# A two-layer hybrid encoder in fp32: first gate/up tile in step with the input, last down tile and final norm in two halves of the tokens

## The chip, the cores and the metric

The kernel runs on one core of one Trainium2 chip. The metric is the device time of one execution in microseconds (us), the median of several runs. Engines are named by the profile's letters: PE is TensorE (matmuls; PEld its weight loads), ACT is ScalarE, DVE is VectorE, POOL is GpSimd, SP is SyncE, which issues the DMAs.

## The reference

One sequence of 512 tokens of 1024 features goes through two layers and a final norm. Four mixers run side by side in a layer: a short convolution, an RWKV-7 scan in both directions, retention, and latent attention (MLA).

```python
for l in range(DEPTH):
    x = x + 0.5 * swiglu(rmsnorm(x, ffn1_norm[l]), ffn1_w_gate[l], ffn1_w_up[l], ffn1_w_down[l])
    u = rmsnorm(x, mix_norm[l]) @ w_in[l]
    ...
    x = x + jnp.concatenate([y_conv, y_rwkv, y_ret, y_mla], axis=-1) @ w_out[l]
    x = x + 0.5 * swiglu(rmsnorm(x, ffn2_norm[l]), ffn2_w_gate[l], ffn2_w_up[l], ffn2_w_down[l])
return rmsnorm(x, final_norm)
```

`swiglu` is `(silu(x @ w_gate) * (x @ w_up)) @ w_down` with 2816 hidden features; `rmsnorm` divides by the root of the mean square over the features and multiplies with a gain.

## The kernel before, in words

x is kept transposed in SBUF as eight tiles x[0] to x[7], each 128 features by 512 tokens. To keep fp32 accuracy every matrix product is made of three matmuls (`mm3`, L336 to L340): high part of the weights times high part of x, high times low, low times high. Weights come from memory in raw fp32 tiles (`load`, a ring of two); `split` (L320) casts a tile to its high part on ACT (L327) and subtracts to get the low part on DVE (L328), each into a ring of two. `norm_part` (L258 on) makes the high part of a scaled x tile, xg, on ACT (L273) and its low part on DVE (L274); `norm_square` squares x on ACT and adds up on POOL; `norm_sum` sums over features on PE (tile st) and takes the inverse root in small DVE steps (`rsqrt`); `norm_spread` broadcasts that row on PE (tile pb) and copies it (rb).

`ffn` (L343) runs, for each half of the hidden features, eleven gate/up tiles (PSUM tiles pg and pu, 24 matmuls each) and eight down tiles (pd, 33 matmuls each). Ahead of it, `setup` issues the first transfers on SP in the order x[0], first 512 columns of the first gate/up tile, x[1] to x[3], the next 512, x[4] to x[7], the other 1024 columns. After the last down tile the final norm squares the last x tile, sums, spreads, and multiplies eight tiles, six on DVE and two on POOL, each followed by its output transfer (main program, L1192 to L1199).

`Mixers.run` makes the projections (`proj`, PSUM tile pj, 24 matmuls of 128x512 each), and for retention's and RWKV's natural layout `proj_nat` (L490 on): pn, 128 tokens by 288 columns, whose weights come as raw pieces of 2 x 576 columns, two such pairs, k tiles 0 to 3 and 4 to 7. `rwkv_inverse` solves small triangular systems: its input NR goes through memory (DMAs s<-NR, L957), comes back as Lb (L959) and Nb (L962); ACT copies Lb reversed into one half of Nb (L960); then DVE runs 31 steps of a product tmpR (L972) and a subtraction from Rb (L974); the result returns through memory, and two sets of small matmuls (psY, psR) use it.

The order of instructions on each engine is not the order of the source: the Tile scheduler sets it (L1271), from its own simulated timeline and priorities (`high_priority` in `split`, `issue_after` where the source wants an order). Each engine then runs its own list in that order.

Of the kernel before, what the change touches and what calls it, by code (L numbers as in the profile page):

```python
# [134 lines left out]
class K:  # L135
# [17 lines left out]
    def setup(self):  # L153
# [15 lines left out]
        first = self.ring.tile([P, 2048], F32, name="w_raw", tag="w_raw", bufs=2)  # L169
        self.first = first  # L170
        for d in range(KD):
            nc.sync.dma_start(self.x[d], I["xT"][:, d, :])
            if d in (0, 3):
                q = 512 * (d // 3)
                nc.sync.dma_start(first[:, q:q + 512], I["gu1"][0, 0][:, q:q + 512])
        nc.sync.dma_start(first[:, 1024:2048], I["gu1"][0, 0][:, 1024:2048])
        self.con_t = per.tile([P, I["con"].shape[1]], F32, name="con_t")
# [80 lines left out]
    def norm_part(self, d, gain, l, square=True):  # L258

        nc, V, A = self.nc, self.nc.vector, self.nc.scalar  # L260
        x = self.x[d]
        if d == 0:
            self.acc = self.ft("acc")
            self.xh, self.xl, self.xo = [], [], []
        if gain == "final_norm":
            self.norm_square(d, True)
            o = self.ft("o")
            A.activation(o, x, AF.Copy, scale=self.v(gain, 0, d))
            self.xo.append(o)
            return  # L270
        hl = self.ht(f"xg{d}", dt=F32R)
        g = self.v(gain, l, d)
        A.activation(hl[:, 0], x, AF.Copy, scale=g)  # L273
        V.scalar_tensor_tensor(hl[:, 1], x, g, hl[:, 0].bitcast(F32), ALU.mult, ALU.subtract)  # L274
        self.xh.append(hl[:, 0])
        self.xl.append(hl[:, 1])
        if square:
            self.norm_square(d)

    def norm_square(self, d, last=False):  # L280
        nc, A, x = self.nc, self.nc.scalar, self.x[d]
        if d == 0:
            A.activation(self.acc, x, AF.Square)
        else:
            self.sq = self.ft("sq")
            A.activation(self.sq, x, AF.Square)
            if d < KD - 1 or not last:
                nc.gpsimd.tensor_tensor(self.acc, self.acc, self.sq, ALU.add)

    def norm_sum(self, last=False):  # L290

        nc = self.nc
        acc = self.acc
        ps = self.ps("st", "a")
        for i, a in enumerate((acc, self.sq)[:1 + last]):
            for tt in range(NT):
                c = NT * i + tt
                m = nc.tensor.matmul(ps[:, c:c + 1], a[:, P * tt:P * tt + P], self.con("ones"), start=True, stop=True)
        rn = self.tmp.tile([P, NT], F32, name="rn", tag="rn")
        ss = ps[:, 0:NT]  # L300
        if last:
            ss = self.tmp.tile([P, NT], F32, name="ss", tag="m_s2", bufs=1)
            nc.vector.tensor_copy(ss, ps[:, 0:NT])
            nc.vector.tensor_tensor(ss, ps[:, NT:2 * NT], ss, ALU.add)
        self.rsqrt(rn, ss, NT, 1.0 / D, EPS)
# [12 lines left out]


# [21 lines left out]


    def ffn(self, l, which, then, between=None):  # L343
        nc, V, A = self.nc, self.nc.vector, self.nc.scalar
        wgu, wdn = self.I[f"gu{which}"], self.I[f"dn{which}"]
        for half in range(2):
            gh, gl = [], []
            for f in range(HALF):
# [5 lines left out]
                pu = self.ps("pu", "b")  # L354
                for o, ps in ((0, pg), (1, pu)):
                    hi, lo = self.split(raw[:, 1024 * o:1024 * o + 1024], 1024, 512 if begin else 1024)
                    if begin and o == 1:
                        with self.tc.issue_after(self.split_hi.ins):
                            for d in range(KD):
                                self.norm_square(d)  # L360
                    for k in range(KD):
# [820 lines left out]
def body(tc, I, out, dbg=None, layers=L):  # L1182
    with ExitStack() as ctx:
        k = K(ctx, tc, I, out, dbg)
        k.setup()
        for d in range(KD):
            k.norm_part(d, "ffn1_norm", 0, square=False)
        for l in range(layers):
            k.ffn(l, 1, ("mix_norm", l), between=k.rope_tables if l == 0 else None)
            Mixers(k, l).run()  # L1190
            k.ffn(l, 2, ("ffn1_norm", l + 1) if l < layers - 1 else ("final_norm", 0))
        k.norm_sum(last=True)  # L1192
        k.norm_spread(last=True)
        for d in range(KD):
            if d in (2, 5):
                k.nc.gpsimd.tensor_tensor(k.x[d], k.xo[d], k.rb, ALU.mult)
            else:
                k.nc.vector.tensor_tensor(k.x[d], k.xo[d], k.pb, ALU.mult)
            k.nc.sync.dma_start(out[:, d, :], k.x[d])  # L1199

# [75 lines left out]
```

## Time and profile before

| what | value |
|---|---|
| median of 3 runs | 2170.99 us (2170.92 to 2171.12) |
| profiled execution | 2169.86 us; its span 2168.1 us |
| PE busy | 2131.3 us, 98% of the span |
| DVE, ACT, POOL busy | 51%, 33%, 6% |
| mean granted PE clock | 0.995 |
| DMA | 204.68 MB, mean 94 GB/s |

The page was taken from one execution. Its busy time of PE is a model (matmuls overlap; one of 512 columns lasts 0.39 us and the next starts 0.23 us later). Times in the timelines are us from the start of the span.

### The profile page before, as it was taken

The page shows a single profiled execution, that of the slowest core. Times are in us where ns is not written, and L with a number is a line of the kernel's source. Part 1 is how long each engine was busy: PE and PEld are TensorE (multiplying, and loading weights), DVE is VectorE, ACT ScalarE, POOL GpSimd, SP SyncE. Part 2 cuts the span into 40 slices and gives each one's busy share as a digit, 9 for nine tenths or more (in the row PEclk, how much of TensorE's full clock was granted, in tenths as well). Part 3 has the DMA queues.
Part 4 walks back from the last instruction along what each step waited for, and adds up shares of the span by engine and source line. Part 5 has one row for each costly group of instructions (what it writes and reads, how often), then busy time and mean ns, then how long its engine had stood idle before and what let it go on. Part 6 is the DMA issues. An engine that isn't in the chain of part 4 may idle for free.

```text
span 2168.1 us, 27576 instructions
## 1 busy us (share of the span) xinstructions
PE 2131.3 (98%) x11316; PEld 1714.9 (79%) x11316; DVE 1113.3 (51%) x1917; ACT 711.6 (33%) x1061; POOL 122.4 (6%) x146
## 2 busy tenths in 40 slices
PE   8999999999999999999999999999999999999997
PEld 7888888788666888888888888887886578888886
DVE  4454445676577543443544444457756865434433
ACT  4222223443233422222322222335323243222232
POOL 2000001000020100000100000010001210000001
PEclk9999999999999999999999999999999999999998
DMA  4223224144002322322322232242330122223222
GB/s 170 97 85 106 98 95 151 61 118 129 20 21 86 116 98 85 117 97 79 106 97 91 94 109 95 92 147 72 116 101 21 64 90 105 91 80 111 97 87 79
DMA packets 65294, 204.68 MB, mean 94 GB/s; under 512 B 26512, under 2 KB 26768, under 8 KB 50960
## 3 DMA queue, kind: packets, MB, share of 16 engines
q1 hardware_dynamic: 65168, 202.93, 28.5%
q8 instruction: 88, 1.44, 0.3%
q14 instruction: 38, 0.31, 0.0%
HBM read 191.37 MB, written 9.44 MB: 93 GB/s over the span
## 4 chain that ended last, share of the span: by engine, by line
PE 93%; DVE 4%; ACT 1%; DMA 1%; issue 1%; SPq 0%; DVEq 0%; ACTq 0%
PE pg L338 7%; PE pg L340 7%; PE pg L339 7%; PE pu L338 7%; PE pd L340 7%; PE pu L339 7%; PE pd L339 7%; PE pd L338 7%; PE pu L340 7%; PE pj L338 4%; PE pj L339 4%; PE pj L340 4%; PE po L338 1%; PE po L339 1%; PE po L340 1%; PE m_pq L758 1%
## 5 line engine op out<-in xcount | busy, mean ns | idle before, releaser
L327 ACT CAST w_hi<-w_raw 128x1024 fp32r<-128x1024 f32 (+4 forms) x446 | 367.4, 836 | 1132.1 <-PE pg L339 308.9
L328 DVE TENSOR_TENSOR w_lo<-w_raw,w_hi 128x1024 fp32r<-128x1024 f32 (+4 forms) x446 | 425.7, 962 | 229.4 <-ACT w_hi L327 220.1
L338 PE MATMUL pg<-xg,w_hi 128*128 128x512 f32 x704 | 275.5, 391 | 6.2 <-ACT w_hi L327 6.2
L340 PE MATMUL pg<-xg,w_lo 128*128 128x512 f32 x704 | 275.0, 391 | 0.0
L339 PE MATMUL pg<-xg,w_hi 128*128 128x512 f32 x704 | 274.9, 390 | 0.0
L338 PE MATMUL pu<-xg,w_hi 128*128 128x512 f32 x704 | 274.1, 389 | 0.4 <-ACT w_hi L327 0.4
L339 PE MATMUL pu<-xg,w_hi 128*128 128x512 f32 x704 | 274.2, 389 | 0.0
L340 PE MATMUL pu<-xg,w_lo 128*128 128x512 f32 x704 | 273.9, 389 | 0.0
L340 PE MATMUL pd<-g,w_lo 128*128 128x512 f32 x704 | 273.9, 389 | 0.0
L338 PE MATMUL pd<-g,w_hi 128*128 128x512 f32 x704 | 273.9, 389 | 0.0
L339 PE MATMUL pd<-g,w_hi 128*128 128x512 f32 x704 | 273.9, 389 | 0.0
L372 DVE TENSOR_TENSOR g<-pu,s 128x512 f32<-128x512 f32 x88 | 60.9, 692 | 274.0 <-PE pu L340 271.2
L369 DVE TENSOR_TENSOR s<-pg,rb 128x512 f32<-128x512 f32 x88 | 60.8, 691 | 206.5 <-PE pg L340 206.4
L338 PEld LDWEIGHTS pg<-xg,w_hi 128*128 128x128 f32 x704 | 132.7, 188 | 33.7 <-ACT w_hi L327 6.2
L340 PEld LDWEIGHTS pg<-xg,w_lo 128*128 128x128 f32 x704 | 132.7, 188 | 28.5 <-DVE w_lo L328 1.0
L339 PEld LDWEIGHTS pg<-xg,w_hi 128*128 128x128 f32 x704 | 132.7, 188 | 28.0 <-DVE xg L274 0.5
L338 PEld LDWEIGHTS pu<-xg,w_hi 128*128 128x128 f32 x704 | 132.2, 188 | 28.1 <-ACT w_hi L327 0.9
L340 PEld LDWEIGHTS pu<-xg,w_lo 128*128 128x128 f32 x704 | 132.2, 188 | 27.5 <-DVE w_lo L328 0.2
L339 PEld LDWEIGHTS pd<-g,w_hi 128*128 128x128 f32 x704 | 132.2, 188 | 27.5
L338 PEld LDWEIGHTS pd<-g,w_hi 128*128 128x128 f32 x704 | 132.2, 188 | 27.4
L340 PEld LDWEIGHTS pd<-g,w_lo 128*128 128x128 f32 x704 | 132.2, 188 | 27.4
L339 PEld LDWEIGHTS pu<-xg,w_hi 128*128 128x128 f32 x704 | 132.2, 188 | 27.3
(294 smaller groups left out, 2706.5 us busy)
## 6 DMA issues: line engine op xcount, KB each, us to landing
w_raw<-gu SPq DMA_DIRECT2D x87, 1024.0 KB, 4.8
w_raw<-dn SPq DMA_DIRECT2D x64, 704.0 KB, 4.2
w_raw<-win SPq DMA_DIRECT2D x22, 1024.0 KB, 5.1
w_raw<-wo SPq DMA_DIRECT2D x32, 256.0 KB, 2.8
xs<-x SPq DMA_DIRECT2D x16, 256.0 KB, 4.7
x<-xs SPq DMA_DIRECT2D x16, 256.0 KB, 5.7
w_raw<-wtv SPq DMA_DIRECT2D x4, 576.0 KB, 4.2
x<-xT SPq DMA_DIRECT2D x8, 256.0 KB, 5.9
```

Source lines behind the costliest of these rows:

```text
L327: self.split_hi = self.nc.scalar.copy(hi[:, s], raw[:, s])
L328: self.nc.vector.tensor_tensor(lo[:, s], raw[:, s], hi[:, s].bitcast(F32), ALU.subtract)
L338: T_.matmul(ps, hi, xh, start=start, stop=False)
L339: T_.matmul(ps, hi, xl, start=False, stop=False)
L340: T_.matmul(ps, lo, xh, start=False, stop=stop)
L369: V.tensor_tensor(s, pg, rb, ALU.mult)
L372: V.tensor_tensor(g, pu, s, ALU.mult)
L758: mm(pq, wq[i][:, P * h:P * h + P], qa[i], start=i == 0, stop=i == 2)
```

## The change

Front: the first tile's gate and up weights come in three pieces each (columns 0 to 256, 256 to 512, 512 to 1024) between the x tiles, and a new function `ffn_begin` runs gate and up in step over k, with `norm_part(k)` just ahead of each use and the squares after the last cast. End: the last down tile of the last layer is computed for tokens 0 to 255 and then 256 to 511, each followed by a new function `end` with that half's sum, norm, products and output transfers (128 KB each). The special cases for the last norm disappear.

```diff
+        pieces = {0: (0, 256), 2: (256, 512), 4: (512, 1024)}
         for d in range(KD):
             nc.sync.dma_start(self.x[d], I["xT"][:, d, :])
-            if d in (0, 3):
-                q = 512 * (d // 3)
-                nc.sync.dma_start(first[:, q:q + 512], I["gu1"][0, 0][:, q:q + 512])
-        nc.sync.dma_start(first[:, 1024:2048], I["gu1"][0, 0][:, 1024:2048])
+            if d in pieces:
+                a, b = pieces[d]
+                for o in (0, 1024):
+                    nc.sync.dma_start(first[:, o + a:o + b], I["gu1"][0, 0][:, o + a:o + b])
...
+    def end(self, c, pd):
...
+        V.scalar_tensor_tensor(t, pd, 0.5, self.rb[:, s], ALU.mult, ALU.mult)
+        V.tensor_tensor(x, x, t, ALU.add)
+        A.activation(sq, x, AF.Square)
+        A.activation(o, x, AF.Copy, scale=self.v("final_norm", 0, d))
+        ps = self.ps("st", "mm")
+        for a in (self.acc, self.sqe):
+            for i in range(2):
+                q = 256 * c + P * i
+                nc.tensor.matmul(ps[:, i:i + 1], a[:, q:q + P], self.con("ones"), start=a is self.acc and i == 0,
+                                 stop=True, skip_group_check=True)
+        rn = self.tmp.tile([P, NT], F32, name="rn", tag="rn")
+        self.rsqrt(rn[:, 0:2], ps[:, 0:2], 2, 1.0 / D, EPS)
+        pb = self.ps("pb", "mm")
+        for i in range(2):
+            nc.tensor.matmul(pb[:, P * i:P * i + P], rn[:, i:i + 1].to_broadcast([P, P]), self.con("ident"),
+                             start=True, stop=True)
+        fb = self.last_t[:, s]
+        A.copy(fb, pb[:, 0:256])
+        for d in range(KD):
+            if d in (1, 4):
+                G.tensor_tensor(self.x[d][:, s], self.xo[d][:, s], fb, ALU.mult)
+            else:
+                V.tensor_tensor(self.x[d][:, s], self.xo[d][:, s], pb[:, 0:256], ALU.mult)
+            nc.sync.dma_start(self.out[:, d, s], self.x[d][:, s])
...
+    def ffn_begin(self, raw, banks):
...
+        for a, b in ((0, 256), (256, 512), (512, 1024)):
+            for o, (hi, lo) in enumerate(w):
+                r = raw[:, 1024 * o + a:1024 * o + b]
+                last = nc.scalar.copy(hi[:, a:b], r)
+                nc.vector.tensor_tensor(lo[:, a:b], r, hi[:, a:b].bitcast(F32), ALU.subtract)
+            for k in range(a // P, b // P):
+                if k:
+                    self.norm_part(k, "ffn1_norm", 0, square=False)
+                for (hi, lo), ps in zip(w, banks):
+                    self.mm3(ps, hi[:, P * k:P * k + P], lo[:, P * k:P * k + P], self.xh[k], self.xl[k],
+                             k == 0, k == KD - 1)
+        with self.tc.issue_after(last.ins):
+            for d in range(KD):
+                self.norm_square(d)
...
+                if half == 1 and d == KD - 1 and then[0] == "final_norm":
+                    w = [self.split(raw[:, P * a:P * b], P * (b - a)) for a, b in ((0, 6), (6, HALF))]
+                    for c in range(2):
+                        pd = self.ps("pd", "a")[:, 0:256]
+                        s = slice(256 * c, 256 * c + 256)
+                        for k in range(HALF):
+                            hi, lo = w[k // 6]
+                            q = P * (k % 6)
+                            self.mm3(pd, hi[:, q:q + P], lo[:, q:q + P], gh[k][:, s], gl[k][:, s], k == 0, k == HALF - 1)
+                        self.end(c, pd)
+                    return
```

The scheduler's order of the instructions changes in places that the diff does not name. Three of them follow. Line numbers of the changed kernel are 25 higher in `split` (L352, L353) and 57 higher in the mixers.

First, the mixers of layer 0 (layer 1 alike): ACT's list around the copy Nb<-Lb of `rwkv_inverse`; the casts of 128x576 are the two pairs of pn's weights. Before:

```order
L327 CAST w_hi<-w_raw 128x576 [waits DMAHW4_49,DVE_49,PE_49]
L327 CAST w_hi<-w_raw 128x576
L684 ACTIVATE m_lat<-pj,vec 128x512 [waits PE_49]
L686 ACTIVATE m_sq<-pj 128x512
L327 CAST w_hi<-w_raw 128x576 [waits DMAHW5_49,DVE_49,PE_49]
L327 CAST w_hi<-w_raw 128x576
L684 ACTIVATE m_lat<-pj,vec 128x512 [waits PE_49]
L686 ACTIVATE m_sq<-pj 128x512
L960 COPY Nb<-Lb 64x1024 [waits DMAHW6_49]
```

With the change:

```order
L352 CAST w_hi<-w_raw 128x576 [waits DMAHW7_49,DVE_49,PE_49]
L352 CAST w_hi<-w_raw 128x576
L741 ACTIVATE m_lat<-pj,vec 128x512 [waits PE_49]
L743 ACTIVATE m_sq<-pj 128x512
L1017 COPY Nb<-Lb 64x1024 [waits DMAHW1_49,DVE_49]
L352 CAST w_hi<-w_raw 128x576 [waits DMAHW0_49,DVE_49,PE_49]
L352 CAST w_hi<-w_raw 128x576
L741 ACTIVATE m_lat<-pj,vec 128x512 [waits PE_49]
L743 ACTIVATE m_sq<-pj 128x512
```

The copy, which waits for a DMA, has moved ahead of the second pair of casts and of the second m_lat and m_sq. On DVE at the same place the list has, with the change:

```order
L353 TENSOR_TENSOR w_lo<-w_raw,w_hi 128x576 [waits DMAHW7_49,PE_49,Activation_49]
L353 TENSOR_TENSOR w_lo<-w_raw,w_hi 128x576 [waits Activation_49]
L1002 TENSOR_TENSOR NR_3056<-psN,con_t 128x8x64 [waits PE_49] x2
L1002 TENSOR_TENSOR NR_3057<-psN,con_t 128x8x64 [waits PE_49] x2
L1029 TENSOR_TENSOR tmpR<-Nb,Rb 128x31 [waits DMAHW2_49,Activation_49,Pool_49]
L1031 TENSOR_TENSOR Rb<-Rb,tmpR 128x31 [waits DVE_49]
L353 TENSOR_TENSOR w_lo<-w_raw,w_hi 128x576 [waits DMAHW0_49,PE_49,Activation_49]
L1029 TENSOR_TENSOR tmpR<-Nb,Rb 128x60 [waits DVE_49]
L353 TENSOR_TENSOR w_lo<-w_raw,w_hi 128x576 [waits Activation_49]
```

Before, the second pair of w_lo stood ahead of the first tmpR, directly behind NR; now each of the two stands behind a product of the inverse.

Second, the start: ACT's list behind the last casts of the first tile's weights (xg_166, xg_175 and xg_184 are made from x[5] to x[7]). Before:

```order
L273 ACTIVATE xg_121<-x_81,vec 128x512 [waits DMAHW2_49]
L327 CAST w_hi<-w_raw 128x512 [waits DMAHW3_49]
L327 CAST w_hi<-w_raw 128x512
L283 ACTIVATE acc<-x_74 128x512
L286 ACTIVATE sq<-x_75 128x512
```

With the change:

```order
L379 CAST w_hi<-w_raw 128x512 [waits DMAHW3_49]
L284 ACTIVATE acc<-x_74 128x512
L287 ACTIVATE sq<-x_75 128x512
L287 ACTIVATE sq<-x_76 128x512
L287 ACTIVATE sq<-x_77 128x512
L287 ACTIVATE sq<-x_78 128x512
L274 ACTIVATE xg_166<-x_79,vec 128x512 [waits DMAHW4_49]
L287 ACTIVATE sq<-x_79 128x512
L274 ACTIVATE xg_175<-x_80,vec 128x512 [waits DMAHW5_49]
L287 ACTIVATE sq<-x_80 128x512
L274 ACTIVATE xg_184<-x_81,vec 128x512 [waits DMAHW6_49]
L287 ACTIVATE sq<-x_81 128x512
```

The squares, which all stood behind the last xg and the last cast, now stand partly between the last three xg.

Third, the end: PE's list, with the change (st is the sum over features, sqe the last tile's square, pb the broadcast):

```order
L365 MATMUL pd<-g_15481,w_lo 128x256
L327 MATMUL st<-con_t,sqe 128x1 [waits Activation_49]
L327 MATMUL st<-con_t,sqe 128x1
L333 MATMUL pb<-con_t,rn 128x128 [waits DVE_49]
L333 MATMUL pb<-con_t,rn 128x128
L327 MATMUL st<-con_t,acc 128x1 x2
L327 MATMUL st<-con_t,sqe 128x1 [waits Activation_49]
L327 MATMUL st<-con_t,sqe 128x1
L333 MATMUL pb<-con_t,rn 128x128 [waits DVE_49,PE_49]
L333 MATMUL pb<-con_t,rn 128x128
```

The first row is the last matmul of the second half; the two st and two pb behind it belong to the first half, and the rest to the second. Before, the list ended with pd, eight st and four pb of all tokens.

## Rows read from the trace of the kernel before

**Rows 1.** The page, part 4: chain that ended last, by engine

```profile
PE 93%; DVE 4%; ACT 1%; DMA 1%; issue 1%; SPq 0%; DVEq 0%; ACTq 0%
```

**Rows 2.** Timelines of ACT and PE at the start (start us, us, engine, line, operation)

```profile
10.15 2.73 ACT L273 ACTIVATE xg<-x,vec 128x512 fp32r<-128x512 f32 x4
13.43 1.14 ACT L327 CAST w_hi<-w_raw 128x512 fp32r<-128x512 f32 x2 [0.55 <-DMA w_raw<-gu]
...
15.01 3.74 ACT L286 ACTIVATE sq<-x 128x512 f32<-128x512 f32 x7
18.66 1.03 ACT L327 CAST w_hi<-w_raw 128x1024 fp32r<-128x1024 f32 x1
...
21.02 0.50 PE L338 MATMUL pu<-xg,w_hi 128*128 128x512 f32 x1 [0.44 <-ACT w_hi L327]
```

**Rows 3.** Windows: stretch, its us, busy PE PEld DVE ACT POOL, PEclk, DMA share, GB/s

```profile
8.00:12.00 4.00, 4.00 (x11) 2.91 (x11) 3.46 (x6) 3.37 (x6) 0.00 (x0) 1.00 1.04 379
```

**Rows 4.** Timelines of ACT, DVE and PE in layer 0's mixers

```profile
460.37 1.25 ACT L327 CAST w_hi<-w_raw 128x576 fp32r<-128x576 f32 x2 [5.42 <-PE pj L339]
...
467.02 1.05 ACT L960 COPY Nb<-Lb 64x1024 f32<-64x1024 f32 x1 [4.33 <-DMA Lb<-s]
...
461.07 1.43 DVE L328 TENSOR_TENSOR w_lo<-w_raw,w_hi 128x576 fp32r<-128x576 f32 x2 [3.92 <-ACT w_hi L327]
468.31 0.21 DVE L972 TENSOR_TENSOR tmpR<-Nb,Rb 128x31 f32<-128x31 f32 x1 [5.81 <-DMA Nb<-s]
...
463.59 0.43 PE L502 MATMUL pn<-w_hi,xg 128*128 128x288 f32 x2
...
475.90 0.50 PE L340 MATMUL pj<-xg,w_lo 128*128 128x512 f32 x1 [1.72 <-DVE w_lo L328]
```

**Rows 5.** The same in layer 1's mixers

```profile
1537.56 1.04 ACT L960 COPY Nb<-Lb 64x1024 f32<-64x1024 f32 x1 [3.19 <-DMA Lb<-s]
...
1535.27 0.43 PE L502 MATMUL pn<-w_hi,xg 128*128 128x288 f32 x2
...
1546.50 0.50 PE L340 MATMUL pj<-xg,w_lo 128*128 128x512 f32 x1 [1.01 <-DVE w_lo L328]
```

**Rows 6.** The page, part 6: DMA issues, count, KB each, us to landing

```profile
w_raw<-win SPq DMA_DIRECT2D x22, 1024.0 KB, 5.1
```

**Rows 7.** Windows around idle PE and at a low clock

```profile
474.00:476.00 2.00, 0.28 (x2) 0.10 (x1) 2.00 (x5) 0.88 (x2) 0.00 (x0) 1.00 0.00 0
...
537.00:543.50 6.50, 6.50 (x20) 5.11 (x19) 0.27 (x1) 0.81 (x3) 2.76 (x5) 0.50 0.18 68
...
1608.50:1612.00 3.50, 3.50 (x11) 2.70 (x10) 0.00 (x0) 0.60 (x1) 1.18 (x1) 0.55 0.07 23
...
2151.00:2155.00 4.00, 1.61 (x14) 1.44 (x13) 2.02 (x7) 1.24 (x2) 0.00 (x0) 0.99 0.00 0
2155.00:2160.00 5.00, 2.07 (x8) 1.78 (x8) 1.91 (x11) 0.58 (x1) 0.39 (x1) 0.50 0.00 0
```

**Rows 8.** Timelines of PE, DVE and SP at the end

```profile
2150.38 0.40 PE L340 MATMUL pd<-g,w_lo 128*128 128x512 f32 x1
2150.61 0.95 PE L298 MATMUL st<-con_t,acc 128*128 128x1 f32 x8
...
2156.84 2.07 PE L246 MATMUL pb<-con_t,rn 128*128 128x128 f32 x8 [2.84 <-DVE rn L241]
...
2154.04 0.16 DVE L303 COPY ss<-st 128x4 f32<-128x4 f32 x1 [1.81 <-PE st L298]
...
2156.62 0.16 DVE L241 SCALAR_TENSOR_TENSOR rn<-rq_t,rq_r 128x4 f32<-128x4 f32 x1
2159.56 3.68 DVE L1198 TENSOR_TENSOR x<-o,pb 128x512 f32<-128x512 f32 x6 [2.78 <-ACT rb L315]
...
2160.28 4.47 SPq L1199 DMA_DIRECT2D out<-x  x8
```

**Rows 9.** Timeline of PE: matmuls of 256 columns (proj_nat, layer 0)

```profile
422.40 0.28 PE L503 MATMUL pn<-w_lo,xg 128*128 128x256 f32 x1
422.52 0.28 PE L504 MATMUL pn<-w_hi,xg 128*128 128x256 f32 x1
```

More of the change, by code (lines that the diff above doesn't have):

```diff
@@ L265, in norm_part @@
         if gain == "final_norm":
-            self.norm_square(d, True)
+            self.norm_square(d)
             o = self.ft("o")
@@ L278, in norm_part, with norm_square @@
             self.norm_square(d)
-    def norm_square(self, d, last=False):
+    def norm_square(self, d):
         nc, A, x = self.nc, self.nc.scalar, self.x[d]
@@ L286, in norm_square, with norm_sum, norm_spread @@
             A.activation(self.sq, x, AF.Square)
-            if d < KD - 1 or not last:
-                nc.gpsimd.tensor_tensor(self.acc, self.acc, self.sq, ALU.add)
-    def norm_sum(self, last=False):
+            nc.gpsimd.tensor_tensor(self.acc, self.acc, self.sq, ALU.add)
+    def norm_sum(self):
         nc = self.nc
-        acc = self.acc
         ps = self.ps("st", "a")
[L295 to L298, printed above, removed]
+        for tt in range(NT):
+            m = nc.tensor.matmul(ps[:, tt:tt + 1], self.acc[:, P * tt:P * tt + P], self.con("ones"), start=True, stop=True)
         rn = self.tmp.tile([P, NT], F32, name="rn", tag="rn")
[L300 to L305, printed above, removed]
+        self.rsqrt(rn, ps[:, 0:NT], NT, 1.0 / D, EPS)
         self.rn = rn
         return m
-    def norm_spread(self, last=False):
-        nc, V = self.nc, self.nc.vector
+    def norm_spread(self):
         pb = self.ps("pb", "a")
@@ L314, in norm_spread @@
         rb = self.tmp.tile([P, T], F32, name="rb", tag="rb", bufs=1)
-        (nc.scalar.copy if last else V.tensor_copy)(rb, pb)
-        self.rb, self.pb = rb, pb
-        return m
+        self.nc.vector.tensor_copy(rb, pb)
+        self.rb = rb
+        return m
+    def end(self, c, pd):
+        nc, V, A, G = self.nc, self.nc.vector, self.nc.scalar, self.nc.gpsimd
+        d, s = KD - 1, slice(256 * c, 256 * c + 256)
+        if c == 0:
+            self.xo.append(self.ft("o"))
+            self.sqe = self.ft("sqe")
+            self.last_t = self.ft("t")
+        t, x, sq, o = self.last_t[:, s], self.x[d][:, s], self.sqe[:, s], self.xo[d][:, s]
+        V.scalar_tensor_tensor(t, pd, 0.5, self.rb[:, s], ALU.mult, ALU.mult)
[22 more added lines that the diff above has]
+            nc.sync.dma_start(self.out[:, d, s], self.x[d][:, s])
     def split(self, raw, n, piece=1024):
@@ L340, in mm3 @@
         T_.matmul(ps, lo, xh, start=False, stop=stop)
+    def ffn_begin(self, raw, banks):
+        nc = self.nc
+        w = []
+        for o in range(2):
+            hi = self.ring.tile([P, 1152], F32R, name="w_hi", tag="w_hi", bufs=2)
+            lo = self.ring.tile([P, 1152], F32R, name="w_lo", tag="w_lo", bufs=2)
+            w.append((hi, lo))
+        for a, b in ((0, 256), (256, 512), (512, 1024)):
[11 more added lines that the diff above has]
+            for d in range(KD):
+                self.norm_square(d)
     def ffn(self, l, which, then, between=None):
@@ L354, in ffn @@
                 pu = self.ps("pu", "b")
[L355 to L360, printed above, removed]
+                if begin:
+                    self.ffn_begin(raw, (pg, pu))
+                for o, ps in ((0, pg), (1, pu)) if not begin else ():
+                    hi, lo = self.split(raw[:, 1024 * o:1024 * o + 1024], 1024)
                     for k in range(KD):
@@ L1185, in body @@
         k.setup()
-        for d in range(KD):
-            k.norm_part(d, "ffn1_norm", 0, square=False)
+        k.norm_part(0, "ffn1_norm", 0, square=False)
         for l in range(layers):
@@ L1191, in body @@
             k.ffn(l, 2, ("ffn1_norm", l + 1) if l < layers - 1 else ("final_norm", 0))
[L1192 to L1199, printed above, removed]
 def pack(i):
```

## The prediction

> **What bounds the kernel now.** I read the chain that ended last first. It is TensorE almost alone, 93% of the span [rows 1]: the 128x512 matmuls stand back to back, one every 0.23 us (the last one begins at 2150.38, what follows it at 2150.61 [rows 8]), so an idle microsecond of TensorE is a microsecond of the result. Then I read the three places where TensorE is not full: the start (timelines of ScalarE and TensorE, DMA share by stretch), the mixers, whose order the scheduler has rewritten although the diff does not touch them, and the end. In [rows 2] the reader is to see that the second gate/up tile's first up matmul, at 21.02, waits for its cast on ScalarE, which had a row of squares to do first; in [rows 3] that the DMA engines were full at that time; in [rows 4, 5] what ScalarE's copy into Nb and VectorE's first product of the inverse wait for, and where TensorE is meanwhile; in [rows 7] the clock around idle TensorE; in [rows 8] the closing chain.
>
> **Front.** Six transfers of 256 and 512 columns replace three; the bytes are the same and the DMA engines are at 1.04 of their share, 379 GB/s [rows 3], so the last piece still lands near 13.4, where the last casts of the first tile begin now [rows 2]. The pieces that land last are now three x tiles: 3 x 262 KB at 379 GB/s are 2.1 us, so the last up piece lands near 11.3. From there ScalarE has two casts (1.14), acc (0.53), four squares (4 x 0.53, from the 3.74 for seven), then xg of tile 5, a square, xg of tile 6, a square, xg of tile 7 (3 x 0.68, from the 2.73 for four; 2 x 0.53): 11.3 + 6.9 = 18.2 [rows 2]. VectorE's low part, taken as long as xg, brings 18.9, and TensorE has 4 or 5 matmuls left: the tile ends near 19.9. Now it ends near 19.9 too, as two matmuls of the next tile lie between its end and the 21.02, with a wait of 0.44. So the early start is spent on waiting for x. As gate and up go in step, both buffers of w_hi come free only at the tile's end; the next two casts of 1.03 [rows 2] follow from about 19.3, and the up matmul of 21.02 comes at 21.3 to 21.5. I take **+0.3**; bounds: the wait at 21.02 and its gap vanish (-0.7), or the second cast lies bare and a half microsecond late (+1.5).
>
> **Middle.** ScalarE's order in both layers' inverse has changed: the copy Nb<-Lb now stands ahead of the second pair of 576-column casts (k tiles 4 to 7 of the weights for the natural projection, pn), and on VectorE the first tmpR and Rb stand ahead of that pair's low parts. Nothing on SyncE ahead of it moved, so the copy still begins at 467.02, when Lb lands, after 4.33 us of idle ScalarE, and ends at 468.07 [rows 4]. What stands behind it on its engine waits with it. Before, those casts ran at 460.37, and TensorE came to k tile 4 at 463.59 without a wait. Now:
> - the first cast of the pair ends at 468.07 + 0.62 (half of 1.25) = 468.7: TensorE stands 5.1 us from 463.59;
> - its low part follows tmpR at 468.31 and Rb (0.21 each, 0.5 with the gaps) and takes 0.72 (half of 1.43): 469.5. TensorE has two high matmuls to fill these 0.8, 0.135 apart by the 0.12 for 256 columns [rows 9]: 0.6 more;
> - the later stall of 1.72 at 475.90, for low weights queued among VectorE's products of the inverse [rows 4], goes, since TensorE comes later. VectorE's row grows there by only the 1.43 that it had done earlier, so nothing is late in its place.
> Layer 0: 5.1 + 0.6 - 1.7 = **+4.0**. Layer 1 likewise: the copy ends at 1537.56 + 1.04 = 1538.60, the cast at 1539.2, against 1535.27: 3.95, plus 0.6, less the stall of 1.01 at 1546.50 [rows 5]: **+3.6**. The weight buffer comes free some 8 us later too, but the next load has two projection tiles (2 x 24 x 0.23 us = 11) to land in, so I cost it at nothing; without that cover it would be up to 5.1, the time of such a load [rows 6]. The scheduler has also put psY some 14 projection matmuls (3.2 us) earlier; that only exchanges work.
>
> **The clock** after such gaps. After the 1.72 us of idle around 475 the clock stayed at 1.00, that is 2.4 GHz; at the end, where TensorE is mostly idle from 2151, it was 0.50 from 2155, that is 1.2 GHz. Two stretches in the middle show what a fall costs: 6.5 us at 0.50 lose 3.25, 3.5 us at 0.55 lose 1.6 [rows 7]. Our gaps, 5.7 and 4.6, are nearer the end's idle time than the 1.72. I take the mean of the two prices for layer 0 (2.4) and the smaller for layer 1 (1.6): **+4.0**; bounds 0 and 6.5.
> The Trainium skill (TensorE: Matmul & The Clock Gate, section "Loop structure matters more than you think") warns of loops that wait for data between their matmuls, since the engine then runs cold. By that rule both gaps cost clock and the sum is the 2183.6 below; by the row at 475 alone neither does, and it is 2179.6.
>
> **Tail.** The last down tile becomes 66 matmuls of 256 columns, 0.12 each [rows 9], 7.9 us, for 33 at 0.23, 7.6: +0.3; and four records of half 0's sum over acc (half of the eight in 0.95 [rows 8]) now stand among them: +0.5. Behind the last of them, at T, TensorE's order has half 0's sum over its last square and its broadcast only now, and VectorE's has half 0's six products ahead of half 1's rsqrt. From T, by [rows 8]: 0.5 (four st records), 2.4 (12 small steps of 0.2, as from 2154.04 to 2156.62), 1.05 (half of pb's 2.07), 0.4 (the copy; now 0.65 lie between pb's end and the first product), 2.2 (six products, a little over half of 3.68); then half 1: 2.4, 1.05, 0.4, and from its first product to the end. This last piece is 8.5 now (2159.56 to 2168.1), with 8 transfers issued over 4.47. Half the bytes, as many issues: between 4.3 and 8.5, I take 7.0, nearer the issue row. Sum 17.4, against 17.5 now (2150.61 to 2168.1). With the 0.8 ahead of T: **+0.7**, bounds -2.0 and +2.2.
>
> **Sum.** 0.3 + 4.0 + 3.6 + 4.0 + 0.7 = +12.6 on the profiled execution of 2169.86 (its span 2168.1 and 1.8 around it), which gives 2182.5. That execution is 1.13 under the median of the runs, 2170.99; against the median **2183.6**.
>
> **Rivals.**
> (a) *The middle costs nothing*: Lb lands early, or TensorE finds its casts done. For: the scheduler put the copy there by its own timeline. Against: 4.33 and 3.19 us of idle ScalarE end with that transfer [rows 4, 5], and SyncE's order up to it is as it was. Only front and tail are left: 2170.99 + 1.0 = 2172.
> (b) *Faster*: the first tile follows the input and the halves overlap. In front the tile would end when the last x is in: 13.4 + 0.7 (xg) + 0.7 (low part) + 1.1 (5 matmuls) = 15.9, up to 4.0 gained. At the end only half 1's chain would follow T: half of the 3.4 from 2150.61 to 2154.04, then 2.4 + 1.05 + 0.4 + 7.0: 12.6 with 0.8 ahead of T, 4.1 gained. Together -8.1: 2163. It counts as faster only if the middle costs under 3.8. Against: squares ahead of the last x tiles in ScalarE's order, and half 0's sum behind all of half 1's matmuls in TensorE's.
> The Trainium skill (Perfetto Trace Analysis, section "DMA Optimizations") says that splitting transfers can let some start, and the whole end, sooner if the DMA engines are generally idle. That is rival (b) for the front, about 2163 with the tail; here they are full [rows 3], so its condition fails.
> (c) *The gaps without a fall of the clock*: 12.6 - 4.0 = 8.6: 2179.6.
> (d) *All at the dear end*: 1.5 + 7.6 + 6.5 + 2.2 = 17.8: 2188.8.
>
> **How the numbers follow.** Forecast 0.58; (c) 0.16; (d) or near it 0.08; (a) 0.12; (b) 0.06. The first three are slower by over 0.2%, 0.82. A difference within 0.2%, 4.3 us, is about what a measurement of this kernel cannot tell from no change: (a) falls there, 0.12. The range runs from between (a) and (c), 2175, to (d), 2189, and leaves (a) and (b) out.
>
> **What would show it.** In the timelines of the changed kernel: ScalarE's Nb<-Lb near 467 with the casts of 576 behind it; TensorE's pn waiting some 5 us for a cast, in both layers; a low clock right behind; no wait of 1.7 us near 476. In front: the second tile's up matmul not before 21. At the end: 17 to 19 us from the last pd to the end, with 12 small VectorE steps between two rows of products. The prediction is wrong if pn does not wait (then (a)), or if half 0's output goes out while half 1's matmuls still run (then (b)).

## The result, and the profile after

| what | before | with the change |
|---|---|---|
| median of the runs | 2171.05 us (2169.84 to 2172.71, 6 runs) | 2185.76 us (2181.60 to 2188.01, 6 runs) |
| ratio of the times, 95% interval | 1 | 1.0066 (1.0053 to 1.0079) |
| profiled execution, its span | 2169.86, 2168.1 us | 2181.6, 2179.8 us |
| mean granted PE clock of that execution | 0.995 | 0.993 |

The change makes the kernel 0.66% slower, 14.7 us between the medians. The profiled execution with the change is the fastest of its six, 4.2 us under their median; where the traces are compared below, 11.7 us of span are to be found. The other five have a mean clock of 0.990 to 0.992; 0.002 of 2180 us is 4.4 us, about what parts this execution from the median. One run of e2 below, at 2375.69 us with a mean clock of 0.847 (0.991 to 0.995 in its nine others), is left out of its median.

The chain that ended last is still TensorE, with 92% of the span for the 93% of [rows 1]. The profile after, page part 4:

```profile
PE 92%; DVE 4%; ACT 1%; DMA 1%; issue 1%; SPq 0%; DVEq 0%; ACTq 0%
```

**The start**, which answers to [rows 2]: timelines of ACT, DVE, POOL and PE after (start us, us, engine, line, operation, count; in brackets the idle time before it and what ended it). The last line is of the kernel before, ACT.

```profile
13.18 2.18 ACT L287 ACTIVATE sq<-x 128x512 f32<-128x512 f32 x4
...
17.53 0.71 ACT L274 ACTIVATE xg<-x,vec 128x512 fp32r<-128x512 f32 x1
...
21.10 1.99 ACT L352 CAST w_hi<-w_raw 128x1024 fp32r<-128x1024 f32 x2 [2.33 <-PE pg L364]
...
10.89 1.42 DVE L275 SCALAR_TENSOR_TENSOR xg<-x,vec,xg 128x512 fp32r<-128x512 f32 x2
...
16.01 4.50 DVE L275 SCALAR_TENSOR_TENSOR xg<-x,vec,xg 128x512 fp32r<-128x512 f32 x3 [2.49 <-ACT xg L274]
...
13.88 11.35 POOL L288 TENSOR_TENSOR acc<-acc,sq 128x512 f32<-128x512 f32 x7 [13.42 <-ACT sq L287]
...
13.74 0.59 PE L365 MATMUL pg<-xg,w_lo 128*128 128x512 f32 x1
14.17 0.40 PE L363 MATMUL pg<-xg,w_hi 128*128 128x512 f32 x1
...
20.14 0.39 PE L363 MATMUL pu<-xg,w_hi 128*128 128x512 f32 x1
20.56 0.50 PE L364 MATMUL pg<-xg,w_hi 128*128 128x512 f32 x1
...
21.37 0.40 PE L365 MATMUL pu<-xg,w_lo 128*128 128x512 f32 x1
...
23.14 0.50 PE L363 MATMUL pu<-xg,w_hi 128*128 128x512 f32 x1 [0.21 <-ACT w_hi L352]
...
19.92 1.05 ACT L327 CAST w_hi<-w_raw 128x1024 fp32r<-128x1024 f32 x1 [0.23 <-PE pu L339]
```

ScalarE does what was forecast: four squares, then the last three xg between squares, the last done at 18.24. The surprise is VectorE's row at 16.01: three low parts in 4.50 us, 1.50 each, where the same instruction took 0.71 at 10.89. They end at 20.51; only then does the first of the tile's last four matmuls start, at 20.56, and the last one at 21.37 (19.72 before). TensorE itself had nothing to spare by then: its matmuls stand 0.43 us apart, as at half clock, until 14.17 (until 11.12 before), and from there to 20.14 0.23 apart without a wait. ScalarE then idles 2.33 us for the weight buffers, and the second tile's first up matmul comes at 23.14 instead of 21.02. From there on the whole first feed-forward block runs 2.67 us later than before.

**The mixers**, which answer to [rows 4, 5]: timelines of ACT, DVE and PE after, layer 0, then ACT and PE of layer 1.

```profile
469.47 1.04 ACT L1017 COPY Nb<-Lb 64x1024 f32<-64x1024 f32 x1 [11.84 <-DMA Lb<-s]
470.53 1.24 ACT L352 CAST w_hi<-w_raw 128x576 fp32r<-128x576 f32 x2
...
470.59 0.21 DVE L1029 TENSOR_TENSOR tmpR<-Nb,Rb 128x31 f32<-128x31 f32 x1 [10.76 <-ACT Nb L1017]
...
471.24 0.76 DVE L353 TENSOR_TENSOR w_lo<-w_raw,w_hi 128x576 fp32r<-128x576 f32 x1 [0.19 <-ACT w_hi L352]
...
471.26 0.61 PE L559 MATMUL pn<-w_hi,xg 128*128 128x288 f32 x2 [4.83 <-ACT w_hi L352]
472.05 0.61 PE L560 MATMUL pn<-w_lo,xg 128*128 128x288 f32 x1 [0.18 <-DVE w_lo L353]
...
472.69 0.44 PE L559 MATMUL pn<-w_hi,xg 128*128 128x288 f32 x1
472.93 0.44 PE L560 MATMUL pn<-w_lo,xg 128*128 128x288 f32 x1
...
1544.07 1.04 ACT L1017 COPY Nb<-Lb 64x1024 f32<-64x1024 f32 x1 [10.99 <-DMA Lb<-s]
...
1545.86 0.53 PE L559 MATMUL pn<-w_hi,xg 128*128 128x288 f32 x2 [3.98 <-ACT w_hi L352]
```

The copy waits for its DMA with the casts of 576 behind it, and TensorE waits for the casts: 4.83 us in layer 0, 3.98 in layer 1. Behind the gap the matmuls stand 0.24 us apart (472.69, 472.93), and 0.13 from 475.2 on. The waits of TensorE between 24 and 2140 us (engine, line, releaser: us in total, times, longest) show these as the largest of all, and the two waits of pj for w_lo, 1.72 and 1.01 in [rows 4, 5], are gone from the list:

```profile
PE pn L559 <- ACT w_hi L352: 9.8, 4, 4.8
PE m_sc L838 <- ACT m_p L843: 4.6, 3, 1.7
```

**The clock and the DMA engines**: windows after, columns as in [rows 3].

```profile
8.00:12.00 4.00, 3.44 (x8) 2.48 (x8) 3.14 (x6) 3.83 (x7) 0.00 (x0) 1.00 1.02 376
...
471.55:474.95 3.40, 3.22 (x14) 2.90 (x14) 3.26 (x8) 1.30 (x3) 1.28 (x1) 0.50 0.31 70
543.25:546.60 3.35, 3.35 (x9) 2.11 (x8) 1.71 (x3) 1.83 (x3) 0.00 (x0) 0.50 0.02 5
1546.80:1550.10 3.30, 3.30 (x14) 3.30 (x15) 3.13 (x7) 0.66 (x2) 1.28 (x1) 0.50 0.50 132
1741.40:1744.70 3.30, 3.30 (x8) 1.45 (x6) 3.30 (x11) 1.48 (x4) 1.27 (x1) 0.50 0.00 0
```

The clock column reads 1.00 in the first row, although the matmuls there stand 0.43 us apart; at the start the spacing is the better guide. Two of the falls to 0.50, that is 1.2 GHz, stand directly behind the new gaps. Of the falls in [rows 7] the long one (537.10 to 543.80 at 0.50) is here one of half its length at 543, and the one at 1608 (1608.90 to 1612.20 at 0.50) isn't there, but one at 1741 is. As an estimate, half of a stretch at 0.50 is lost: 1.7 us for each of the four, 6.7 together, and 5.0 for the two of before.

**The end**, which answers to [rows 8]: timelines of PE, DVE and SP after.

```profile
2161.99 0.28 PE L365 MATMUL pd<-g,w_lo 128*128 128x256 f32 x1
...
2166.96 2.08 DVE L341 TENSOR_TENSOR x<-o,pb 128x256 f32<-128x256 f32 x6 [1.72 <-ACT t L336]
2168.95 0.15 DVE L236 TENSOR_SCALAR rq_v<-st 128x2 f32<-128x2 f32 x1
...
2173.05 2.07 DVE L341 TENSOR_TENSOR x<-o,pb 128x256 f32<-128x256 f32 x6 [1.78 <-ACT t L336]
...
2167.41 9.86 SPq L342 DMA_DIRECT2D out<-x  x16
```

The last pd starts 11.61 us later than before (2150.38). From there to the end of the span it takes 17.8 us, against 17.7 before. The halves follow one another: half 0's six products at 2166.96, then half 1's inverse root from 2168.95, then its products at 2173.05 and 6.75 us more.

### The profile page after: what moved, and what is told of

Same layout as the page of the kernel before. It is cut to its first block, busy times and chain, and to the rows that moved or that the text cites. A ratio compares the mean times of both kernels' runs of the same rounds, so it can differ in the third digit from the quotient of the medians.

```text
span 2179.8 us, 27695 instructions
## 1 busy us (share of the span) xinstructions
PE 2136.9 (98%) x11349; PEld 1718.4 (79%) x11349; DVE 1121.5 (51%) x1937; ACT 712.6 (33%) x1066; POOL 123.3 (6%) x148
## 4 chain that ended last, share of the span: by engine, by line
PE 92%; DVE 4%; ACT 1%; DMA 1%; issue 1%; SPq 0%; DVEq 0%; ACTq 0%
PE pg L365 7%; PE pg L363 7%; PE pd L365 7%; PE pu L365 7%; PE pd L363 7%; PE pu L363 7%; PE pd L364 7%; PE pg L364 7%; PE pu L364 7%; PE pj L363 4%; PE pj L364 4%; PE pj L365 4%; PE po L364 1%; PE po L363 1%; PE po L365 1%; PE m_pq L815 1%
## 5 line engine op out<-in xcount | busy, mean ns | idle before, releaser
L352 ACT CAST w_hi<-w_raw 128x1024 fp32r<-128x1024 f32 (+4 forms) x442 | 365.0, 838 | 1116.7 <-PE pg L364 319.4
L353 DVE TENSOR_TENSOR w_lo<-w_raw,w_hi 128x1024 fp32r<-128x1024 f32 (+4 forms) x442 | 423.3, 965 | 216.7 <-ACT w_hi L352 208.5
L364 PE MATMUL pd<-g,w_hi 128*128 128x512 f32 (+1 forms) x715 | 275.8, 386 | 0.0
L363 PE MATMUL pd<-g,w_hi 128*128 128x512 f32 (+1 forms) x715 | 275.8, 386 | 0.0
L365 PE MATMUL pd<-g,w_lo 128*128 128x512 f32 (+1 forms) x715 | 275.6, 386 | 0.0
```

The lines of the kernel that those rows point to most:

```text
L352: self.split_hi = self.nc.scalar.copy(hi[:, s], raw[:, s])
L353: self.nc.vector.tensor_tensor(lo[:, s], raw[:, s], hi[:, s].bitcast(F32), ALU.subtract)
L363: T_.matmul(ps, hi, xh, start=start, stop=False)
L364: T_.matmul(ps, hi, xl, start=False, stop=False)
L365: T_.matmul(ps, lo, xh, start=False, stop=stop)
```

## The experiments

Before runs beside each on the same chip: medians 2171.23 (17 runs, e1 to e4), 2170.23 (12, e5 to e8) and 2171.04 (28, e9 to e11).

**e1: the front alone.** The kernel before with `setup` and `ffn_begin` of the change, and the end as before.

```diff
+        pieces = {0: (0, 256), 2: (256, 512), 4: (512, 1024)}
...
+    def ffn_begin(self, raw, banks):
```

> The kernel before with the change's front alone; the tail is as before, and the scheduler again puts the copy Nb<-Lb ahead of the second pair of 576-column casts in both layers. My theory: the front costs 2.7 us where it stands (a longer stretch of half-clock matmuls, then two casts that nothing covers) and, through the order in the mixers, another 8 to 12: 2181 to 2187 against 2171. Rival (the tail carries the loss, the order in the mixers is harmless): 2171 to 2174.

Measured: 2181.53 us (2180.72 to 2184.85, 4 runs), ratio 1.0053 (1.0038 to 1.0068). The first feed-forward block is 2.70 us late, and pn waits 4.8 and 4.1 us: the front's edit alone makes the scheduler put the copy ahead of the casts, some 450 us later in the program. Up to the end of the program ScalarE's list is that of the changed kernel, instruction for instruction. Why the scheduler's simulated timeline tips there was not found out.

**e2: the end alone.** The change with `setup` and the first tile put back.

```diff
-    def ffn_begin(self, raw, banks):
...
+            if d in (0, 3):
+                q = 512 * (d // 3)
+                nc.sync.dma_start(first[:, q:q + 512], I["gu1"][0, 0][:, q:q + 512])
```

> The kernel before with the change's tail alone; front as before, and in the mixers the casts stand ahead of the copy as they did before. My theory: about 1 us slower, 2172, with pn not waiting. Rival (the tail carries the loss): 2180 or more.

Measured: 2172.02 us (2168.38 to 2174.54, nine runs), ratio 1.0003 (0.9994 to 1.0013). The order in the mixers is as before, and the last pd to the end takes 17.6 us. The end by itself costs 0.8 us between the medians, and by the interval anything from 1.3 us gained to 2.8 lost.

**e3: the order alone.** The kernel before, with the second pair of 576-column casts tied behind the copy.

```diff
-                A.copy(Nb[64:128], Lb[64:128, ::-1])
+                self.nb_copy = A.copy(Nb[64:128], Lb[64:128, ::-1])
...
+                if o and n == W + 32:
+                    with self.tc.issue_after(self.nb_copy.ins):
+                        pieces.append(k.split(raw, half, 2 * n))
```

> The kernel before with one thing changed: in both layers ScalarE must run the copy Nb<-Lb ahead of the second pair of 576-column casts; front and tail are those of before, VectorE keeps its order of before. My theory: pn waits about 5 us in layer 0 and 4 us in layer 1 for the cast, the clock falls to half behind both gaps, and the later waits of 1.7 and 1.0 us go: 6 to 12 us slower, 2177 to 2183. Rival (the order is harmless, TensorE would find other work or the transfer lands early): within 2 us of before.

Measured: 2176.99 us (2176.04 to 2179.33, 8 runs), ratio 1.003 (1.0019 to 1.0041): 5.8 us slower, just under the 6 to 12 expected. No other edit is made, but the scheduler moves more than the casts: on ScalarE one copy some 50 us later, on VectorE and TensorE a number of instructions behind the gap. ACT and PE, layer 0:

```profile
466.80 1.04 ACT L967 COPY Nb<-Lb 64x1024 f32<-64x1024 f32 x1 [5.13 <-DMA Lb<-s]
467.86 1.24 ACT L327 CAST w_hi<-w_raw 128x576 fp32r<-128x576 f32 x2
...
468.59 1.09 PE L509 MATMUL pn<-w_hi,xg 128*128 128x288 f32 x3 [3.34 <-ACT w_hi L327]
```

The gap is 3.3 us here (2.2 in layer 1), shorter than in the changed kernel, because in this version's order TensorE has more matmuls of k tiles 0 to 3 to do first. The order makes the wait; its size depends on what TensorE has left. A fall of the clock stands behind each gap here too (0.50 at 468.15 to 471.55 and 1543.35 to 1546.70), and in e1 (471.15 to 474.50, 1546.35 to 1549.70); in e9 below, without the gaps, the clock is 1.00 at 465 to 480 and at 1538 to 1555. Not every wait has one: behind e5's of 2.3 us in layer 0 it is 1.00 (471.20 to 474.50).

**e4: the copy off ScalarE.** The change with the copy on GpSimd.

```diff
-                A.copy(Nb[64:128], Lb[64:128, ::-1])
+                G.tensor_copy(Nb[64:128], Lb[64:128, ::-1])
```

> The changed kernel with the copy Nb<-Lb on GpSimd, so that nothing on ScalarE waits for the transfer; the casts and their low parts then stand ahead of the inverse's products again. My theory: the gaps in pn vanish, front and tail stay: 3 to 5 us over before, 2174 to 2176. Rival: the loss in the middle has another cause and stays: 2182 to 2187.

Measured: 2193.0 us (2186.79 to 2198.81, 4 runs), ratio 1.0102 (1.0077 to 1.0127). A miss that decides nothing: pn's longest wait is 0.5 us, as the theory has it, but the scheduler rearranged the attention and the scan as well, with new waits (m_ptp for m_p 4.3 us in two) and a mean clock of 0.984 to 0.991.

**e5: the order put back, one edge.** The change, with the copy tied behind the second cast of 576.

```diff
+            if n == W + 32:
+                self.tc.add_manual_dep(self.nb_copy.ins, k.split_hi.ins.name, ...
```

> The changed kernel with one edge more: in both layers ScalarE must run the second pair of 576-column casts ahead of the copy Nb<-Lb, as it did before the change; front and tail are the change's, and VectorE's low parts are back ahead of the inverse's products. My theory: the gaps in pn vanish and 2.7 us of the front and 1 us of the tail are left: 2173 to 2177. Rival (the mixers lose for another reason that the change brought): 2180 to 2186. The run with the copy on GpSimd could not tell, since the scheduler changed much else there.

Measured: 2181.01 us (2179.82 to 2181.22, 4 runs), ratio 1.0051 (1.0033 to 1.0069): a miss. The longest of the waits of PE in layer 0 (24 to 1484 us):

```profile
PE pn L563 <- ACT m_sq L747: 2.3, 1, 2.3
```

The casts no longer wait, but now the second m_lat and m_sq stand behind the copy. They read the projection's PSUM tile pj, and until they have read it pn has no bank to go to. I had freed one of the instructions behind the copy and left the other two there.

**e6: the front with a warm clock.** The front of e1 with the edge of e5, and nine matmuls of zeros ahead of the first tile, whose results nobody reads.

```diff
+        wz = self.ft("wz", dt=F32R)
+        nc.vector.memset(wz.bitcast(F32), 0.0)
+        for i in range(9):
+            nc.tensor.matmul(wp, wz[:, 0:P], wz, start=True, stop=True)
```

> The change's front alone, with the order in the mixers put back as in the run before this one, and nine matmuls on a tile of zeros at the very start, whose output nobody reads, so that TensorE works before the first data. My theory: the first tile's end at 21.6 is late by some 1.6 us because its matmuls run at half clock until 14.2 instead of 11.3; with the extra matmuls they run at full clock by 9 or sooner, the tile ends at 20.0 to 20.4 and the second tile's first up matmul moves from 23.1 to about 21.6. Rival (x arrives too late for more, behind the squares on ScalarE): tile end and up matmul stay within 0.4 of 21.6 and 23.1.

Measured: 2180.96 us (one run). With the change the first tile's matmuls run at half clock until 14.2 us (11.1 before); here they stand 0.23 us apart from 6.8 us on. The first block is still 2.61 us late, and VectorE's three low parts still take 4.45. The profiled execution of e5 says the same without an edit: it has the change's front, its matmuls stand 0.23 apart from 10.3 on until they wait, and the block is 2.65 us late. The clock alone does not make the front's loss; with it mended, TensorE waits for xg and its low parts instead. PE of e5:

```profile
10.30 0.40 PE L364 MATMUL pg<-xg,w_hi 128*128 128x512 f32 x1
...
16.07 0.50 PE L363 MATMUL pg<-xg,w_hi 128*128 128x512 f32 x1 [0.61 <-ACT xg L274]
...
21.36 0.40 PE L365 MATMUL pu<-xg,w_lo 128*128 128x512 f32 x1
```

**e7: the squares out of the way.** e6, with all squares behind the last xg and five of them behind the second tile's first cast.

```diff
-        with self.tc.issue_after(last.ins):
+        with self.tc.issue_after(self.xg_ins.ins):
             for d in range(KD):
                 self.norm_square(d)
...
+                    for i in self.late_sq:
+                        self.tc.add_manual_dep(i.ins, self.split_hi.ins.name, ...
```

> As the run before this one, and with the squares behind the last x tile's high part on ScalarE, the last five of them also behind the second tile's first gate cast. My theory: now neither the clock nor the squares hold the first tile back; it ends at 16.8 to 18, and the whole is 1 to 3 us faster than before, 2168 to 2170. Rival (the transfers bound the front): the tile ends at 19 or later and the time is that of before or up to 1 us more.

Measured: 2178.54 us (2177.78 to 2183.94, 4 runs), ratio 1.0047 (1.0031 to 1.0063); the total misses, since the middle is still that of e5. The front is what it was for: the first block is 0.68 us late, not 2.61. DVE, POOL, PE and ACT:

```profile
13.52 1.42 DVE L281 SCALAR_TENSOR_TENSOR xg<-x,vec,xg 128x512 fp32r<-128x512 f32 x2
...
16.93 2.64 POOL L295 TENSOR_TENSOR acc<-acc,sq 128x512 f32<-128x512 f32 x2 [16.47 <-ACT sq L293]
...
18.59 0.39 PE L347 MATMUL pu<-xg,w_lo 128*128 128x512 f32 x1
20.45 0.50 PE L345 MATMUL pg<-xg,w_hi 128*128 128x512 f32 x1 [1.47 <-ACT w_hi L334]
...
19.35 1.04 ACT L334 CAST w_hi<-w_raw 128x1024 fp32r<-128x1024 f32 x1 [1.99 <-DMA w_raw<-gu]
```

With GpSimd idle the low parts take 0.71 each again, and the tile's last matmul starts at 18.59 (21.29 in e6). The edit takes away two things at once: the adds beside the low parts, and the squares between the last xg on ScalarE, the last of which now ends at 15.80 (18.23 in e6). But nothing is won against the kernel before: the second tile's weights land only then, and their cast has no matmuls to hide it. The first tile can end early; the second tile's load sets the time.

**e8: half 0's end inside half 1's matmuls.** e2, with half 0's sum behind the 12th matmul of half 1, its broadcast right behind the last, and half 1's transfers from SP and ACT in turn.

```diff
+                    st0, rn0 = self.end(0, pds[0], m1)
+                    with self.tc.issue_after(st0.ins):
+                        m2 = down(1, range(4, HALF))
+                    self.end2(0, rn0, m2)
...
+            (nc.scalar if c and d % 2 else nc.sync).dma_start(self.out[:, d, s], self.x[d][:, s])
```

> The kernel before with the change's tail alone, but with half 0's sum put behind the twelfth matmul of half 1 and its broadcast right behind the last one, and half 1's transfers issued from SyncE and ScalarE in turn. My theory: half 0's chain then runs under half 1's matmuls; from the last pd to the end 12 to 14.5 us instead of 17.7: 2167 to 2170. Rival (half 0's chain was hidden anyway, or issue and landing of 16 transfers set the end): 17 us or more, 2171 to 2173.

Measured: 2169.1 us (2166.6 to 2172.42, 10 runs), ratio 0.9995 (0.9986 to 1.0005). From the last pd to the end 14.2 us, 3.4 less than in e2: half 1's first product comes 8.4 us behind the last pd (11.1 in e2), and no transfer of half 1 stands ahead of that, so 2.7 us of it belong to the order in which half 0's inverse root runs beside matmuls. The rest comes behind, where the second queue is. Counted from the last tile's first matmul, which now has the sum among its matmuls, the end takes 22.9 us for 25.8.

**e9: the order put back, both edges.** The change, with the copy behind the cast and behind the last m_sq.

```diff
+            if n == W + 32:
+                for i in (k.split_hi, self.last_sq):
+                    self.tc.add_manual_dep(self.nb_copy.ins, i.ins.name, ...
```

> The changed kernel with two edges: ScalarE must run the second pair of 576-column casts, and the last square of the latent projections (m_sq) too, ahead of the copy Nb<-Lb. With the casts alone put back, pn waited 2.3 and 1.4 us for that square instead, which holds the PSUM tile that pn needs and had come to stand behind the copy. My theory, now that the copy blocks whatever stands behind it: with both ahead of it the waits in pn vanish (only those of the kernel before are left), and 2.7 us of the front, 1 us of the tail and 0 to 2 us of the later order are left: 2174 to 2177. Rival (the later order of the mixers is itself worse, whatever the copy does): 2179 or more.

Measured: 2174.09 us (2172.54 to 2176.07, 10 runs), ratio 1.0012 (1.0003 to 1.0022). Of the loss 3.05 us are left (0.7 to 4.8 by the interval), the size of the front's 2.7 and the end's 1. ACT in layer 0, and the waits of PE there:

```profile
463.40 1.25 ACT L352 CAST w_hi<-w_raw 128x576 fp32r<-128x576 f32 x2 [5.42 <-PE pj L364]
464.55 0.69 ACT L746 ACTIVATE m_lat<-pj,vec 128x512 f32<-128x512 f32 x1
465.13 0.59 ACT L748 ACTIVATE m_sq<-pj 128x512 f32<-128x512 f32 x1
469.65 1.05 ACT L1022 COPY Nb<-Lb 64x1024 f32<-64x1024 f32 x1 [3.93 <-DMA Lb<-s]
```

```profile
PE pj L365 <- DVE w_lo L353: 1.6, 1, 1.6
...
PE pn L564 <- ACT w_hi L352: 0.5, 1, 0.5
```

The copy runs at the same time as in the changed kernel (469.65, 469.47) and waits for the same DMA. On ScalarE up to there only what stands behind it is different, and with that the gap is gone and the stall of pj is back. Later in the program the scheduler moved other instructions as well.

**e10: the end's queue as well.** e8, with half 0's six products behind half 1's inverse root on VectorE, and six of half 1's transfers from ACT.

```diff
+                    with self.tc.issue_after(self.rs_ins.ins):
+                        self.end3(0, pb0)
+                    self.end3(1, self.end2(1, rn1))
```

> As the tail with half 0's sum put into half 1's matmuls, and half 0's six products on VectorE now behind half 1's rsqrt, with six of half 1's transfers issued from ScalarE. My theory: half 1's rsqrt no longer waits 2 us behind those products; from the last pd to the end 12.2 to 13.5 us instead of 14.2: 1 to 2 us less than that run, 2167 to 2168.5. Rival (the issue and landing of the transfers bounds it): 14 us or more again, 2169.

Measured: 2168.39 us (2165.62 to 2170.14, 10 runs), ratio 0.999 (0.9981 to 0.9999). From the last pd (2154.33) to the end of the span (2168.4) 14.1 us, a miss: the rival's "14 us or more". DVE:

```profile
2156.93 0.54 DVE L236 TENSOR_SCALAR rq_r<-rq_v 128x2 int32<-128x2 int32 x1
2157.50 0.65 DVE L237 TENSOR_SCALAR rq_r<-rq_r 128x2 int32<-128x2 int32 x1
```

Half 1's inverse root ends 5.6 us behind the last pd for 6.6 in e8, although two of its steps take 0.54 and 0.65 us, for 0.17 in e8, beside GpSimd's products of half 0. But from there to the end it is 8.5 us for 7.7, with most outputs of both halves leaving together; what holds the end there was not found out. The total lies below both kernels, by 2.7 us against the one before (0.2 to 4.1 by the interval).

**e11: all mended.** The change with e9's edges, e7's squares and zero matmuls, e10's end, and a constant's transfer moved behind the second tile's weights.

```diff
+        self.second = self.load(I["gu1"][0, 1], 2048)
         self.con_t = per.tile([P, I["con"].shape[1]], F32, name="con_t")
```

> The change with all that the runs point to: the two edges in the mixers, the squares behind the last x tile's high part (five of them behind the next gate cast), the nine matmuls on zeros at the start, the transfer of the constants behind the second gate/up tile's, and the tail of the run before. My theory: the front 0.5 to 2 us ahead of before, the middle within 1.5 us of it, the tail 3 to 4 us shorter: 2165 to 2168.5 against 2171. Rival (the order in the mixers takes it back): 2169 to 2173.

Measured: 2169.2 us (2166.24 to 2176.45, 12 runs), ratio 0.9993 (0.9984 to 1.0001). This is above the 2165 to 2168.5 expected. Against the kernel before no difference is shown, and none against e10. In the trace the mended front is there (the first down tile starts at 130.78, at 131.37 before), but 0.6 us can't be seen in the times.

## Why the prediction was right, and where it was not

The forecast, slower at 2183.6 us, came true at 2185.76. The working of the parts was less good than the sum: the front's term was much too small, the clock's too large, and in the profiled execution the two errors cancel, which is luck. There the parts measure 2.7 + 3.8 + 4.2 + 1.0 (the shift of TensorE's matmuls before and behind each layer's mixers, and at the last pd) and 0.1 behind the last pd, with rounding the 11.7 us of span, for the 12.6 of the sum.

- **Front: +2.7 for +0.3**, beyond the bound of 1.5. The step that failed is "VectorE's low part, taken as long as xg". ScalarE's row came true within 0.1 us, but the low parts took 1.50 us each beside GpSimd's adds of the squares, which the prediction did not price, and ended at 20.51 for 18.9. In e5 and e6, where the clock was up early, the block is as late, so the clock alone is not the cause. It is a second row that ends almost as late, though. "4 or 5 matmuls left" took TensorE to have kept pace with the input, but at half clock until 14.17 it had ten left at 18.9. With the low parts on time its own row would have ended the tile at 21.06 in this execution (20.14 and four steps of 0.23), for the 21.37 that came. When the clock rises is not the edit's doing: with the front of before it rose at 10.0 in e2 and at 13.8 in e8, with the change's at 10.3 in e5. No run takes away the adds alone; e7 also moves the squares off ScalarE's path and starts with a warm clock, so its 0.68 us is not the price of the adds by itself. The rest came as the bound had it, the second tile's casts lying bare. One reading of [rows 2] was off: the cast before the matmul at 21.02 (19.92) waited 0.23 us for TensorE to release its buffer, not for squares. The Trainium skill (Perfetto Trace Analysis, section "DMA Optimizations") says that splitting transfers may let the whole end sooner if the DMA engines are generally idle; they stood at 1.02 of their share, 376 GB/s, so the condition failed, as the prediction said.
- **Middle, the mechanism: right.** The copy, the casts behind it, pn's gap in both layers, and the stalls of pj gone, each as forecast: 4.83 + 0.18 us for 5.1 + 0.6 in layer 0, 3.98 + 0.26 for 3.95 + 0.6 in layer 1. e3 makes the gaps in the kernel before with one edge, at 5.8 us; e9 takes them out of the changed kernel with two and leaves 3.05 of the 14.7 us. So rival (a) falls. How much of those totals is the copy's alone is not parted, since the scheduler moved other instructions in both. What the prediction did not price is that m_lat and m_sq had moved behind the copy too, which is why e5 failed.
- **The clock: +4.0 was too much for the profiled execution.** Both gaps end in a fall, as the forecast had it. The Trainium skill (TensorE: Matmul & The Clock Gate, section "Loop structure matters more than you think") says that long waits for data between matmuls leave TensorE cold; the trace agrees, with 0.50 granted for some 3.4 us behind each of the two gaps. These two falls cost 1.7 us each by the estimate above, near the smaller price of the prediction and not its 2.4: 3.4 for 4.0. But the prediction took the falls of [rows 7] to stay as they were, and they did not: elsewhere 3.3 us are lost for 5.0 before, so 1.7 net. The waits of TensorE grew by 3.1 us in layer 0 and by 2.1 in layer 1 (sums over all its waits there), which leaves 0.7 and 2.1 of the 3.8 and 4.2. The clock's 1.7 fall in layer 1; 0.7 and 0.4 are not traced to a row. At the median the loss is 3 us larger than in this execution, at a lower mean clock; at which places those executions lost it no trace shows.
- **End: right**, +1.0 ahead of the last pd's start and 0.1 behind it for the forecast +0.7. The order of the halves decided, as rival (b) feared for itself: in e8 and e10, where half 0's sum is taken among half 1's matmuls, it is some 3.5 us from the last pd shorter, 3 of them net of the longer last tile.
- **The parts do not add up to the last microsecond**: e1 and e2 are 10.3 and 0.8 us slower than before, the change 14.7. The intervals of e1 and of the change overlap, and what separates them further is not settled.

## What to carry to other kernels

Where a scheduler sets the order, an edit at one end can rearrange a place that the diff does not touch; so compare each engine's list of before and after first. On an engine that runs its list in order, as ScalarE does here, an instruction that waits for a DMA makes everything behind it wait, in e5 even reads that held a PSUM bank: free all of what stands behind it, not the first. And work in halves paid here only where the first half's small steps stood among the second half's matmuls.

## What was not expected of the hardware

**VectorE slows down beside GpSimd.** The two-input operation of 128x512 takes 0.71 us alone and 1.50 beside GpSimd's adds, which themselves take 1.62 each (11.35 for seven) where VectorE works beside some of them, and 1.32 where it is idle (2.64 for two, e7). The Trainium skill (SBUF — State Buffer, section "Who interferes with whom") says that a VectorE instruction with two SBUF inputs contends with a GpSimd instruction that reads SBUF; the trace agrees, with these numbers. The kernel before had it already, unread, in the low parts of the second tile: timelines of DVE and POOL of the kernel before.

```profile
19.73 3.44 DVE L328 TENSOR_TENSOR w_lo<-w_raw,w_hi 128x1024 fp32r<-128x1024 f32 x2 [4.35 <-ACT w_hi L327]
27.65 1.23 DVE L328 TENSOR_TENSOR w_lo<-w_raw,w_hi 128x1024 fp32r<-128x1024 f32 x1 [4.47 <-ACT w_hi L327]
...
15.71 11.35 POOL L288 TENSOR_TENSOR acc<-acc,sq 128x512 f32<-128x512 f32 x7 [15.26 <-ACT sq L286]
```

They take 1.72 us each while GpSimd adds, and 1.23 once it has ended at 27.06. That row would have shown that the low part can't be taken as long as xg.

**The falls of the clock move.** The one at 537 to 543.5 of [rows 7] comes at 543 to 546.5 after, behind the same small matmuls, and the one at 1608 is absent. The full clock at the start moves too, and with it the first down tile: 131.15 in e2, 132.59 in e8, with the same front. The times of one kernel differ likewise: the 28 of the kernel before lie between 2166.59 and 2174.91 us, more than most parts of this change are worth, and only many runs tell 2 us from that.
